# MLP up projection of a two-layer diffusion trunk: two separate two-bank PSUM tiles for blocks A and B in place of the two halves of one

## The chip, the cores and the metric

The kernel runs on one NeuronCore of one Trainium2 chip, in one launch. The metric is the device time of one execution in microseconds. Three runs of the kernel before took 1686.57 us in the median (1686.32 to 1688.69). All matrix products are made in three passes of float32r operands (below), all sums in float32.

## The reference

Two layers of a trunk process 512 latent tokens and 128 context tokens of width 1024. Each layer has a token mixer (differential attention in layer 0, neighbourhood attention in layer 1) and an MLP with squared ReLU. Each sub-layer is modulated, gated and closed by a layer norm; the part that matters here is the MLP:

```python
def modulate(x, shift, scale):
    return x * (1 + scale) + shift

def sq_relu_mlp(h, w1, w2):
    return jnp.square(jax.nn.relu(h @ w1)) @ w2

# in each layer, for context (xp) and latent tokens (xs) alike
y = sq_relu_mlp(modulate(xs, ms[:, 3], ms[:, 4]), w_mlp1[i], w_mlp2[i])
xs = layer_norm(ALPHA * xs + ms[:, 5] * y, ln_g[i, 1], ln_b[i, 1])
```

w1 is 1024 x 4096 and w2 4096 x 1024. The modulation's vectors (shift, scale, gate) are SiLU(cond) times a 1024 x 6144 matrix per layer.

## The kernel before

**Three passes.** Every float32 product is split in hi and lo parts, and `mm3` (lines 119 to 123) issues three matmuls for one 128-deep step: hi x hi, hi x lo, lo x hi. The results build up in PSUM. A 128x512 float32 result is one bank of 2 KB per partition.

**PSUM.** There are eight banks. Two pools, `psA` and `psB` (lines 77 and 78), hold one buffer of `[128, 1024]` each, two banks, under the tag S; `S()` (line 149) hands out the two in turn by a counter `turn`. The other four banks are a ring of one-bank tiles M. `halves()` (line 145) takes one S tile and returns its two banks as two blocks. The framework makes waits from what is read and written in a tile.

**Weights.** They come in quarters of a chunk: 256 rows by 512 columns, a 512 KB DMA on SyncE's queue into one of three raw tiles rw. `conv` (line 184) makes the hi part on ScalarE (wh, line 190) and the lo part (wl, line 192) on VectorE for one half, and for the other on VectorE or, from the first down projection on, on GpSimd. Five converted quarters fit (RING). When the last matmul has used a quarter (`used`, `done`), the next conversion is issued.

**The MLP** is `rest` (line 1200). Four groups (`gr`) of 1024 hidden features each are done in order: up projection in two chunks (`c`) of 512 features, then the down projection of the group. An up chunk has four blocks of 128 features over the 512 latent tokens (`ff`, features on the partitions), and one block C for the 128 context tokens over all 512 features (`nat`). The first two blocks run one after the other into M tiles. The other two, here A and B, and C are staggered (`STAGGER`, line 38): pairs (block, quarter) in the order A0 B0 C0 A1 A2 B1 C1 A3 B2 C2 B3 C3. A quarter of A, B or C is six matmuls. The first chunk of each layer is done otherwise, so seven chunks per layer take this path.

**Read-out.** When a block's quarter 3 is issued, `act` (line 1216) evacuates it: ScalarE makes relu (r, line 1213), VectorE squares it with a second read of the PSUM block (r, line 1214), then `split` makes the operands of the down projection: uhi on ScalarE (line 128), ulo on VectorE (line 129). C goes the same way into rc, and is transposed later.

**Fillers on VectorE.** In layer 0, VectorE also works out layer 1's modulation: 96 products jk of 128x1024 (line 289), two for each 512 KB tile wm that SyncE loads two tiles ahead. `aside` (line 1239) steps this generator after a block's read-out, and the down projection steps it too. In group 0 `aside` scales rows of X instead (line 1041).

**Order.** TensorE's order is that of the code, since it is scheduled by hand. The framework orders the other engines' instructions and the queues by itself.

Of the kernel before, what the change touches and what calls it, by code (L numbers as in the profile page):

```python
# [66 lines left out]
class Net:  # L67
# [1132 lines left out]
    def rest(self, l, X, first):  # L1200
# [3 lines left out]
        with self.tc.tile_pool(name=f"mlp{l}", bufs=1) as pool:  # L1204
# [11 lines left out]
            def act(us, k, src, cs):  # L1216
                r = pool.tile([P, NL], F32, tag="r", name=self.nm("r"), bufs=2)[:, : cs.stop - cs.start]
                op = square(r, src)
                self.split(us[0][:, k, cs], us[1][:, k, cs], r)
                return op  # L1220

            def act_ctx(us, c, src):
                r = pool.tile([P, NL], F32, tag="rc", name=self.nm("rc"), bufs=1)
                op = square(r, src)

                def tr():
                    tp = self.M()
                    for k in range(4):
                        nc.tensor.transpose(tp[:, P * k : P * k + P], r[:, P * k : P * k + P], self.idf)
                    ks = slice(4 * c, 4 * c + 4)  # L1230
                    self.split(us[0][:, ks, NL:], us[1][:, ks, NL:], tp.rearrange("p (a b) -> p a b", b=P))

                wait.append(tr)
                return op
# [4 lines left out]
            def aside(op, x=0):  # L1239
                if gr and x < 2:  # L1240
                    next(mods, None)
                if gr == 0:
                    self.scale(X, len(vec), vec_g, op)
                    vec.append(0)
                elif gr == 1 and len(vec) < 2 * NTT:
                    self.shift(X, len(vec) - NTT, vec_b)
                    vec.append(0)

            for gr in range(4):
                us = [pool.tile([P, KT, NT], F32R, tag=t, name=self.nm(t)) for t in ("uhi", "ulo")]  # L1250
                for c in range(2):
                    n = C0 + 8 + 4 * gr + c
                    if gr == 0 and c == 0:
                        for f in range(4):
                            act(us, f, first[f], slice(0, CUT))
                        for f in range(4):
                            m = self.M()[:, : NT - CUT]
                            self.ff(n, f, CUT, NT, m)
                            act(us, f, m, slice(CUT, NT))
                        gate = self.gate_tiles(pool, l, 1)  # L1260
                        vec_g, vec_b = self.ln_tiles(pool, l, 0)
                        st = self.sml.tile([P, NTT, 2, 6], F32, tag="st", name=self.nm("st"), bufs=2)
                        continue
                    for f in range(2):
                        m = self.M()
                        self.ff(n, f, 0, NL, m)
                        aside(act(us, 4 * c + f, m, slice(0, NL)))
                    while wait:
                        wait.pop()()
                    ms = [*self.halves(), self.M()]  # L1270
                    for x, k in STAGGER:
                        if x < 2:
                            self.ff(n, 2 + x, 0, NL, ms[x], 2 * k, 2 * k + 2)
                        else:
                            self.nat(hT, 4, n, ms[x], 0, 512, 2 * k, 2 * k + 2, k == 0)
                        if k == 3:
                            aside(act(us, 4 * c + 2 + x, ms[x], slice(0, NL)) if x < 2 else act_ctx(us, c, ms[x]), x)
                if gr < 3:
                    for n in range(2):
                        self.pool_lo = 1  # L1280
                        for t in range(NTT):
                            m = self.M()
                            self.nat(us, t, C0 + 10 + 4 * gr + n, m, 0, 512)
                            if n == 0 and t == 1:
                                wait.pop()()
                            self.add_gated_sb(pool, X, t, n, m, gate, gr == 0, nc.gpsimd)
                            next(mods, None)
# [173 lines left out]
```

## Time and profile before

| what | value |
|---|---|
| median of three runs | 1686.57 us (1686.32 to 1688.69) |
| the profiled execution | 1688.53 us, of it span 1686.8 us |
| TensorE busy (PE) / weight loads (PEld) | 1606.5 us (95%) / 1388.0 us (82%) |
| VectorE / ScalarE / GpSimd busy | 1081.2 / 687.9 / 293.0 us |
| mean granted TensorE clock | 0.989 |

The span is counted from the first to the last instruction. In the profile's rows "L121 PE MATMUL S<-hhi,wh" is the matmul of line 121 into a tile S from tiles hhi and wh; "128*128 128x512" is the array and the result. A group's row ends with busy time, mean time of one in ns, and the idle time of the engine ahead of its instructions with the one that ended it. Rows of the order of time begin with start and length in us; the idle time ahead stands in brackets. A matmul's length (0.39 us for 512 columns) is longer than the distance of two starts, as they are pipelined; pace is read from the starts.

### The profile page before, as it was taken

How to read it: one execution, taken by the hardware profiler on the slowest of the kernel's cores; microseconds unless marked ns; L12 is line 12 of the kernel's file. 1: busy time of each engine (PE TensorE's matmuls, PEld its weight loads, DVE VectorE, ACT ScalarE, POOL GpSimd, SP SyncE). 2: the span in 40 equal slices, each digit the busy share in tenths (PEclk: the TensorE clock that was granted, in tenths of full speed). 3: DMA queues.
4: the chain of work that ended last, by engine and by line, in shares of the span. 5: the costliest groups of instructions: out<-in, count | busy, mean ns of one | idle time of the engine just before them, and what ended most of it. 6: DMA issues, size and time to landing. Idle time of an engine off the chain costs nothing. (4 is left out here: it accounts for less than half of the span.)

```text
span 1686.8 us, 23934 instructions
## 1 busy us (share of the span) xinstructions
PE 1606.5 (95%) x9074; PEld 1388.0 (82%) x9074; DVE 1081.2 (64%) x2174; ACT 687.9 (41%) x1398; POOL 293.0 (17%) x236
## 2 busy tenths in 40 slices
PE   8999999899999999999999999998899999999997
PEld 6888989787977778787788999987797878778776
DVE  4788778875659779688366777768654632232336
ACT  2556545744722322313245655554552232231322
POOL 0000000000003246255101011000000224324310
PEclk9999999999999999999999999999999999999999
DMA  8432234331424445444225343444041322221211
GB/s 343 147 122 95 90 118 150 115 113 55 164 86 162 168 142 177 151 161 143 71 88 175 121 136 122 137 137 162 15 149 63 113 72 78 75 75 51 100 51 62
DMA packets 60932, 200.59 MB, mean 119 GB/s; under 512 B 7716, under 2 KB 14354, under 8 KB 59922
## 3 DMA queue, kind: packets, MB, share of 16 engines
q1 hardware_dynamic: 55186, 175.09, 30.4%
q0 software_dynamic: 5632, 23.99, 4.0%
q8 instruction: 71, 1.16, 0.3%
q14 instruction: 43, 0.35, 0.1%
HBM read 186.41 MB, written 7.40 MB: 115 GB/s over the span
## 5 line engine op out<-in xcount | busy, mean ns | idle before, releaser
L190 ACT CAST wh<-rw 128x1024 fp32r<-128x1024 f32 x192 | 199.7, 1053 | 398.1 <-PE M L123 318.3
L192 DVE TENSOR_TENSOR wl<-rw,wh 128x512 fp32r<-128x512 f32 x288 | 224.0, 813 | 148.0 <-ACT wh L190 146.9
L121 PE MATMUL M<-wh,hhi 128*128 128x256 f32 (+1 forms) x752 | 244.4, 325 | 6.4 <-DVE red L266 2.2
L121 PE MATMUL M<-wh,uhi 128*128 128x512 f32 x640 | 250.1, 391 | 0.0
L123 PE MATMUL M<-wh,ulo 128*128 128x512 f32 x640 | 249.1, 389 | 0.0
L122 PE MATMUL M<-wl,uhi 128*128 128x512 f32 x640 | 249.1, 389 | 0.0
L123 PE MATMUL M<-wh,hlo 128*128 128x256 f32 (+1 forms) x752 | 240.2, 319 | 5.8 <-DVE hlo L129 5.6
L122 PE MATMUL M<-wl,hhi 128*128 128x256 f32 (+1 forms) x752 | 239.3, 318 | 0.0
L192 POOL TENSOR_TENSOR wl<-rw,wh 128x512 fp32r<-128x512 f32 x96 | 173.9, 1821 | 324.1 <-ACT wh L190 323.7
L123 PE MATMUL M<-hhi,wl 128*128 128x320 f32 (+2 forms) x544 | 189.0, 347 | 1.9 <-DVE wl L192 1.9
L121 PE MATMUL M<-hhi,wh 128*128 128x320 f32 (+2 forms) x544 | 189.5, 348 | 0.8 <-ACT wh L190 0.6
L122 PE MATMUL M<-hlo,wh 128*128 128x320 f32 (+2 forms) x544 | 188.3, 346 | 0.3 <-DVE hlo L129 0.3
L123 PEld LDWEIGHTS M<-wh,hlo 128*128 128x128 f32 x752 | 144.9, 193 | 18.6 <-DVE hlo L129 9.9
L121 PEld LDWEIGHTS M<-wh,hhi 128*128 128x128 f32 x752 | 145.1, 193 | 18.1 <-DVE red L266 2.5
L122 PEld LDWEIGHTS M<-wl,hhi 128*128 128x128 f32 x752 | 145.3, 193 | 8.6
L1111 DVE TENSOR_TENSOR tmp<-M,gate 128x512 f32<-128x512 f32 x80 | 55.0, 687 | 134.8 <-PE M L123 132.3
L289 DVE SCALAR_TENSOR_TENSOR jk<-wm,cb 128x1024 bf16<-128x1024 f32 x96 | 140.5, 1464 | 1.2
L123 PEld LDWEIGHTS M<-wh,ulo 128*128 128x128 f32 x640 | 120.1, 188 | 25.1
L122 PEld LDWEIGHTS M<-wl,uhi 128*128 128x128 f32 x640 | 120.2, 188 | 24.6
L121 PEld LDWEIGHTS M<-wh,uhi 128*128 128x128 f32 x640 | 120.2, 188 | 24.7
L121 PE MATMUL S<-hhi,wh 128*128 128x512 f32 (+1 forms) x288 | 108.4, 376 | 21.1 <-DVE r L1214 21.1
L123 PEld LDWEIGHTS M<-hhi,wl 128*128 128x128 f32 x544 | 102.7, 189 | 12.5 <-DVE wl L192 3.9
(280 smaller groups left out, 2869.9 us busy)
## 6 DMA issues: line engine op xcount, KB each, us to landing
rw<-in_w SPq DMA_DIRECT2D x192, 512.0 KB, 4.0
wm<-in_wmodT SPq DMA_DIRECT2D x48, 512.0 KB, 3.5
rw<-in_wmod SPq DMA_DIRECT2D x32, 512.0 KB, 4.5
E<-in_bias POOLq DMA_DIRECT2D x32, 384.0 KB, 4.9
wm<-in_wmod SPq DMA_DIRECT2D x7, 1024.0 KB, 11.4
Q<-Q SPq DMA_DIRECT2D x16, 320.0 KB, 3.7
gate<-gates POOLq DMA_DIRECT2D x6, 512.0 KB, 5.1
X<-in_xT SPq DMA_DIRECT2D x8, 320.0 KB, 11.7
```

What stands on the lines that cost most here:

```text
L121: te.matmul(out, sh, mh, start=start, stop=False)
L122: te.matmul(out, sh, ml, start=False, stop=False)
L123: te.matmul(out, sl, mh, start=False, stop=stop)
L190: keep(nc.scalar.copy(hi, r))
L192: keep(eng.tensor_tensor(lo[:, k], r[:, k], hi[:, k], ALU.subtract))
L289: op = nc.vector.scalar_tensor_tensor(jk, ws[t], 1.0, cb[:, x, :], ALU.mult, ALU.mult, accum_out=mc[:, t, x : x + 1])
L1111: nc.vector.tensor_tensor(tmp, m, gate[t // 4][:, cs], ALU.mult)
```

## The change

```diff
@@ -1267,7 +1267,7 @@
                     while wait:
                         wait.pop()()
-                    ms = [*self.halves(), self.M()]
+                    ms = [self.S()[:, :512], self.S()[:, :512], self.M()]
                     for x, k in STAGGER:
                         if x < 2:
                             self.ff(n, 2 + x, 0, NL, ms[x], 2 * k, 2 * k + 2)
```

Before, A and B were the two banks of one S tile, and successive chunks took the two S buffers in turn. Now A is the first bank of one S buffer and B the first bank of the other, in every chunk. Matmuls, read-outs, conversions and loads are the same in number, size and operands, and TensorE's order is the same.

On TensorE, at the end of A's quarter 3 and the start of B's quarter 2 (second chunk of group 2 in layer 0; S with its number is the tile), with the semaphores waited for. Before:

```order
L121 MATMUL S_7099<-hhi,wh_6980 128x512
L122 MATMUL S_7099<-hlo,wh_6980 128x512
L123 MATMUL S_7099<-hhi,wl_6981 128x512
L121 MATMUL S_7099<-hhi,wh_6944 128x512 [waits DVE_49]
L122 MATMUL S_7099<-hlo,wh_6944 128x512
L123 MATMUL S_7099<-hhi,wl_6945 128x512
```

Now:

```order
L121 MATMUL S_7103<-hhi,wh_6984 128x512
L122 MATMUL S_7103<-hlo,wh_6984 128x512
L123 MATMUL S_7103<-hhi,wl_6985 128x512
L121 MATMUL S_7104<-hhi,wh_6948 128x512
L122 MATMUL S_7104<-hlo,wh_6948 128x512
L123 MATMUL S_7104<-hhi,wl_6949 128x512
```

The order is the same; A and B have two tile numbers, and the wait for VectorE at B's quarter 2 is gone. The same holds in all 14 chunks. Some later matmuls name a wait for a wl, or for VectorE at a down projection's first matmul, which they did not name before, because the wait at B's quarter 2 had covered it.

On VectorE, from A's square to rc in the same chunk. Before:

```order
L1214 SCALAR_TENSOR_TENSOR r_7163<-S_7099,r_7163 128x512
L129 TENSOR_TENSOR ulo_6820<-r_7163,uhi_6819 128x512
L289 SCALAR_TENSOR_TENSOR jk_7168,mc_103<-wm_7054,cb 128x1024
L289 SCALAR_TENSOR_TENSOR jk_7170,mc_103<-wm_7054,cb 128x1024
L192 TENSOR_TENSOR wl_7187<-rw_7015,wh_7186 128x512
L1214 SCALAR_TENSOR_TENSOR r_7199<-S_7099,r_7199 128x512
L129 TENSOR_TENSOR ulo_6820<-r_7199,uhi_6819 128x512
L289 SCALAR_TENSOR_TENSOR jk_7204,mc_103<-wm_7090,cb 128x1024
L192 TENSOR_TENSOR wl_7217<-rw_7124,wh_7216 128x512
L289 SCALAR_TENSOR_TENSOR jk_7206,mc_103<-wm_7090,cb 128x1024
L1214 SCALAR_TENSOR_TENSOR rc_7223<-M_7100,rc_7223 128x512
```

Now:

```order
L1214 SCALAR_TENSOR_TENSOR r_7168<-S_7103,r_7168 128x512
L129 TENSOR_TENSOR ulo_6823<-r_7168,uhi_6822 128x512
L289 SCALAR_TENSOR_TENSOR jk_7173,mc_103<-wm_7058,cb 128x1024
L192 TENSOR_TENSOR wl_7192<-rw_7019,wh_7191 128x512
L289 SCALAR_TENSOR_TENSOR jk_7175,mc_103<-wm_7058,cb 128x1024
L1214 SCALAR_TENSOR_TENSOR r_7204<-S_7104,r_7204 128x512
L192 TENSOR_TENSOR wl_7222<-rw_7129,wh_7221 128x512
L129 TENSOR_TENSOR ulo_6823<-r_7204,uhi_6822 128x512
L289 SCALAR_TENSOR_TENSOR jk_7209,mc_103<-wm_7094,cb 128x1024
L1214 SCALAR_TENSOR_TENSOR rc_7228<-M_7105,rc_7228 128x512
L289 SCALAR_TENSOR_TENSOR jk_7211,mc_103<-wm_7094,cb 128x1024
```

The first wl has moved ahead of the second jk, the second wl ahead of B's ulo, and rc ahead of the last jk. The chunks of groups 1 and 2 in layer 0 change in this way, and the first of group 3 in a like one, with the last steps of the modulation; in groups 1 and 2, ScalarE's cast wh for that second wl moves ahead of B's uhi, and on SyncE's queue a load of rw ahead of a load of wm. All other chunks keep their order.

## The prediction

> **What bounds the kernel now.** I read the page first (shares of the span and costliest groups), then the list of waits, then the order of time around one of the waits. The first three rows are the page's, the next two the list of waits, the last the page of line 1214, in the part on who waited for it.
>
> ```profile
> PE 1606.5 (95%) x9074; PEld 1388.0 (82%) x9074; DVE 1081.2 (64%) x2174; ACT 687.9 (41%) x1398; POOL 293.0 (17%) x236
> ...
> L121 PE MATMUL S<-hhi,wh 128*128 128x512 f32 (+1 forms) x288 | 108.4, 376 | 21.1 <-DVE r L1214 21.1
> L123 PE MATMUL M<-hhi,wl 128*128 128x320 f32 (+2 forms) x544 | 189.0, 347 | 1.9 <-DVE wl L192 1.9
> ...
> PEld S L121 <- DVE r L1214: 27.0, 14, 2.1
> PE S L121 <- DVE r L1214: 21.1, 14, 1.7
> ```
>
> TensorE is busy for 95% of the span; the next engine, VectorE, for 64%. What TensorE does not do at full pace is what the span is made of. The largest idle time that section 5 shows before any of its groups is 21.1 us before matmuls into a tile S, all ended by VectorE's squared ReLU (line 1214), in 14 places. Fourteen is the number of staggered pieces: 4 MLP groups x 2 chunks x 2 layers, less the first chunk of each layer, which takes another path. The order of time shows one such place in layer 0:
>
> ```profile
> 478.40 0.39 PE L122 MATMUL S<-hlo,wh 128*128 128x512 f32 x1
> 478.63 0.39 PE L123 MATMUL S<-hhi,wl 128*128 128x512 f32 x1
> ...
> 479.12 0.60 ACT L1213 ACTIVATE r<-S 128x512 f32<-128x512 f32 x1 [0.36 <-PE S L123]
> 480.00 0.68 DVE L1214 SCALAR_TENSOR_TENSOR r<-S,r 128x512 f32<-128x512 f32 x1
> ...
> 480.74 0.50 PE L121 MATMUL S<-hhi,wh 128*128 128x512 f32 x1 [1.72 <-DVE r L1214]
> 481.07 0.39 PE L122 MATMUL S<-hlo,wh 128*128 128x512 f32 x1
> ```
>
> Block A's last matmul starts at 478.63. ScalarE and VectorE read A's half of S, and only when VectorE is through (480.68) does block B go on (480.74). B's data need none of it: its weights are those that A's third step has already used, and its half of S is written by nobody else. So what B waits for is the tile, not a value.
>
> **The change part by part.** (1) *What it removes.* Matmuls of 512 columns start 0.23 us apart (478.40, 478.63). Here 2.11 us pass (478.63 to 480.74), so 1.88 are lost, and the matmul behind starts 0.33 later instead of 0.23, another 0.10: 1.98 us. The idle time shown (1.72) is less, since a matmul's own 0.39 overlaps the next one's start. A second kind of place, here in the third group of layer 0:
>
> ```profile
> 707.60 0.39 PE L123 MATMUL S<-hhi,wl 128*128 128x512 f32 x1
> 709.47 0.50 PE L121 MATMUL S<-hhi,wh 128*128 128x512 f32 x1 [1.47 <-DVE r L1214]
> 709.80 0.39 PE L122 MATMUL S<-hlo,wh 128*128 128x512 f32 x1
> ```
>
> 1.87 - 0.23 = 1.64, and 0.33 - 0.23 = 0.10: 1.74 us. Two of the 14 are of the first kind (the first group of each layer, where a weight conversion stood ahead of the square on VectorE) and 12 of the second: 2 x 1.72 + 12 x 1.47 = 21.1, the idle time in the group's row, so the count is right. The loss is 2 x 1.98 + 12 x 1.74 = **24.8 us**. With two tiles B's third step has no reason to wait, as the rows of the new order show. All of it lies on the path, because TensorE has nothing else to do there: its instructions stand in one fixed order.
>
> (2) *What it adds.* Each block asks for a tile of its own and leaves its second bank unused. Twice as many requests per chunk, on the same two buffers: A always takes one, B the other, where whole chunks alternated before. So A's first step must wait until A of the chunk before is read out. Between B's last step and its next first step lie 6 matmuls of C, 48 of the next chunk's first two blocks and 6 of A, 60 x 0.23 = 13.8 us; B's read-out ends, by the slowest chain worked out below, 3.9 us after B's last start. Cost nothing; if the cover were gone, at most the 1.74 us per chunk that stand there now. The requests at the end of layer 0 (the early V blocks) change buffers, since 14 requests flip the turn by an even number where 7 flipped it by an odd one. Between their read-out and the next work on these buffers, the first scores, the written order has seven other blocks of matmuls: nothing.
>
> (3) *What it moves.* Layer 1 keeps its order on VectorE, ScalarE and the queues. In layer 0 five chunks (two each in groups 1 and 2, the first of group 3) carry the modulation's products (jk, in pairs), and there the order changes: conversion (wl) moves ahead of the second jk, and B's ulo stands behind the next wl. On SyncE's queue a weight load (rw) moves ahead of a modulation load (wm) in four of them; wm is loaded two pairs ahead of its use, and no jk of this trace waits for a DMA, so that costs nothing (without this cover a load's median 3.5 us each, section 6 of the page). This is where a gain can be lost, so I work through the tightest case, a chunk that is followed by the down projection (709.47 on), which needs ulo at once:
>
> ```profile
> 708.72 0.69 DVE L1214 SCALAR_TENSOR_TENSOR r<-S,r 128x512 f32<-128x512 f32 x1 [0.23 <-ACT r L1213]
> 710.10 0.69 DVE L129 TENSOR_TENSOR ulo<-r,uhi 128x512 fp32r<-128x512 f32 x1 [0.69 <-ACT uhi L128]
> 710.71 1.22 DVE L289 SCALAR_TENSOR_TENSOR jk<-wm,cb 128x1024 bf16<-128x1024 f32 x1
> ...
> 713.65 0.69 DVE L192 TENSOR_TENSOR wl<-rw,wh 128x512 fp32r<-128x512 f32 x1 [0.45 <-ACT wh L190]
> 714.58 0.69 DVE L1214 SCALAR_TENSOR_TENSOR r<-S,r 128x512 f32<-128x512 f32 x1 [0.23 <-ACT r L1213]
> 715.96 0.69 DVE L129 TENSOR_TENSOR ulo<-r,uhi 128x512 fp32r<-128x512 f32 x1 [0.69 <-ACT uhi L128]
> ...
> 717.71 1.77 DVE L192 TENSOR_TENSOR wl<-rw,wh 128x512 fp32r<-128x512 f32 x1
> ...
> 723.00 2.19 DVE L289 SCALAR_TENSOR_TENSOR jk<-wm,cb 128x1024 bf16<-128x1024 f32 x1
> ...
> 712.57 1.05 ACT L190 CAST wh<-rw 128x1024 fp32r<-128x1024 f32 x1 [2.50 <-PE M L123]
> ...
> 713.70 1.81 POOL L192 TENSOR_TENSOR wl<-rw,wh 128x512 fp32r<-128x512 f32 x1 [4.08 <-ACT wh L190]
> 716.95 1.98 POOL L192 TENSOR_TENSOR wl<-rw,wh 128x512 fp32r<-128x512 f32 x1 [1.45 <-ACT wh L190]
> 721.90 2.21 POOL L1119 TENSOR_TENSOR X<-X,tmp 128x512 f32<-128x512 f32 x1 [2.97 <-DVE tmp L1111]
> ...
> 715.04 0.39 PE L121 MATMUL M<-wh,uhi 128*128 128x512 f32 x1
> ...
> 720.26 0.39 PE L123 MATMUL M<-wh,ulo 128*128 128x512 f32 x1
> ```
>
> Three facts: a wl or a jk that starts under a GpSimd instruction lasts until that has ended and then its own time (717.71 and 723.00 above, 1.77 and 2.19 against 0.69 and 1.22). GpSimd converts the other half of each quarter, for 1.8 to 2.0 us. The down projection's matmul on B's ulo starts at 720.26, its weight load one start earlier, at 720.03.
>
> Now take 1.74 us off TensorE's times after 707.60. The cast of 712.57 starts at 710.83 and ends at 711.88. VectorE is through with the first jk at 711.93, does its wl till 712.62; GpSimd converts till 713.7. The second jk starts under it and ends at 713.7 + 1.22 = 714.9; B's square, which could have started at 712.84, ends at 715.6. The next cast, behind C's last step, ends near 714.5, GpSimd's half at 716.5, VectorE's wl behind it at 717.2, then ulo at **717.9**. It is wanted at 720.03 - 1.74 = **718.29**. So 0.4 us are left of what were 3.4 (716.65 against 720.03). I cost this at nothing, but it is thin: if my chain is 1 us short, each of the two such chunks with jk and a down projection behind them (groups 1 and 2) stalls 0.6 us, 1.2 in all; if jk and wl both meet GpSimd once more (about 1 us each), 2 x 1.6 = 3.2. The other three moved chunks are followed by work on older tiles and lie easier. Bounds of this term: 0 to +3.2 us; I take 0.2.
>
> VectorE stays later than before behind such a chunk, but it catches up; the down projection as a whole is unchanged, and TensorE's clock is full in all of it:
>
> ```profile
> 566.66:596.14 29.48, 28.00 (x124) 22.85 (x125) 19.93 (x30) 9.97 (x15) 7.36 (x5) 1.00 0.41 143
> 596.14:680.00 83.86, 82.39 (x365) 67.89 (x365) 73.38 (x88) 18.41 (x23) 45.30 (x23) 1.00 0.48 163
> 1359.68:1389.16 29.48, 28.00 (x125) 22.85 (x125) 9.51 (x14) 9.96 (x15) 7.18 (x5) 1.00 0.21 72
> ```
>
> The columns are the stretch, its length, then busy time of PE, PEld, DVE, ACT and POOL, the granted clock, and the DMA share. From stall to stall of one group (566.66 to 596.14) VectorE works 19.93 of 29.48 us; without the stall 19.93 of 27.74, 72%. In the 83.86 us with the down projection in it, 73.38, 88%, and of 82.12 it would be 89%. So there is room in every stretch of layer 0, and much in layer 1 (9.51 us).
>
> (4) *A wait that stays.* At 544.85 and 547.67 TensorE waits for wl (most of the 1.9 us of the page's third row), behind a run of VectorE work without a pause that begins at 508.76:
>
> ```profile
> 544.15 0.39 PE L122 MATMUL M<-hlo,wh 128*128 128x512 f32 x1
> 544.85 0.50 PE L123 MATMUL M<-hhi,wl 128*128 128x512 f32 x1 [0.31 <-DVE wl L192]
> ...
> 546.11 0.40 PE L122 MATMUL M<-hlo,wh 128*128 128x512 f32 x1
> 547.67 0.50 PE L123 MATMUL M<-hhi,wl 128*128 128x512 f32 x1 [1.16 <-DVE wl L192]
> ...
> 508.76 0.69 DVE L1111 TENSOR_TENSOR tmp<-M,gate 128x512 f32<-128x512 f32 x1 [1.61 <-PE M L123]
> ```
>
> From start to start less 0.23 that is 0.47 and 1.33, with 0.1 behind each 2.0 us. The run begins with VectorE waiting 1.61 us for TensorE; if TensorE comes 1.98 us earlier, all of it does. I leave the wait as it is: bounds -2.0 (it vanishes) and +2.0 (the one gain ahead of it, 1.98, is eaten).
>
> **Sum.** -24.8 + 0.2 = -24.6 us. The profiled execution took 1688.53 us, 1.7 more than its span of 1686.8; the three runs have the median 1686.57. Nothing outside the span changes, so the profile should show a span near 1662.2, and the median should be 1686.57 - 24.6 = **1662.0 us**. The likeliest case's own range is 24.8 less 3.2 and 2.0, to 24.8 plus 2.0: 1659.8 to 1667.0.
>
> **The rivals.** *A, VectorE becomes the bound in the modulation's chunks.* If the new order makes ulo or wl late by as much as the stall was, the five moved chunks of layer 0 give back 5 x 1.74 = 8.7 us: 1662.0 + 8.7 = 1670.7. For it: 0.4 us of slack in the chain above, and the wait at 544.85, which shows that wl can be late. Against it: 28% of VectorE free, and three of the five have no consumer near. Chance 0.09.
>
> *B, nothing gained.* TensorE would find another thing to wait for at the same place, or the wait would stay on the tile: 1686.6. For it speaks little: B's third step uses weights that A's third step used without a wait, and the new order has no wait there. Chance 0.03. The Trainium skill has a case of this kind (TensorE: Matmul & The Clock Gate, section "HAM oscillation — how this bites in real kernels"): in a kernel that kept TensorE fed, adding PSUM double-buffering gave no further gain. By that this change would give nothing; the 14 waits above show that this kernel's TensorE is not fed at these points, so the trace disagrees.
>
> *C, slower: the clock.* Place: the two MLP stages, from which the pauses are taken. The granted clock of TensorE is the last but two of the columns:
>
> ```profile
> 42.00:420.00 378.00, 361.19 (x2612) 321.48 (x2612) 292.40 (x767) 206.43 (x508) 13.85 (x25) 0.97 0.34 112
> 420.00:452.00 32.00, 28.68 (x190) 27.58 (x189) 20.39 (x42) 26.25 (x64) 3.13 (x6) 0.95 0.35 131
> 452.00:850.00 398.00, 385.97 (x1713) 317.35 (x1712) 297.57 (x399) 101.20 (x130) 134.85 (x70) 1.00 0.41 141
> 1236.00:1630.00 394.00, 383.45 (x1717) 317.94 (x1716) 146.56 (x203) 105.56 (x141) 112.83 (x74) 1.00 0.24 83
> ```
>
> For it: the clock is not always full here. If TensorE without pauses were granted 0.95 in these 792 us, as it was from 420 to 452, they would last 792 x (1/0.95 - 1) = 41.7 us longer: 1703.7. It decides at 792 x (1/c - 1) = 24.6, a clock of 0.97. Against it: in the 83.86 us above TensorE runs without a pause but one, at 1.00, and the stages with less are those in which it idles more (361.19 busy of 378, against 385.97 of 398). Chance 0.02. The same page of the Trainium skill (section "What's actually happening") says that idleness throttles the array and activity releases it, and the four rows agree; by that, C can't happen.
>
> **How the numbers follow.** Forecast 0.86, A 0.09, B 0.03, C 0.02. A measurement of this kernel can tell about 0.2%, 3.4 us, from no change. Forecast and A are both faster by far more: 0.95; same 0.03; slower 0.02. The range reaches from a little under the forecast's own low end, 1659.5, to 1668.5, part of the way to A; it leaves out most of A, B and C (0.14) and some of the forecast's edges.
>
> **What would show it.** In the profile after: the row of matmuls into S with its 21.1 us idle before and "DVE r L1214" gone from the waits of PE and PEld; stall-to-stall stretches of one group 27.7 us long instead of 29.48; VectorE's busy time as before. A step is wrong if TensorE shows new waits for "DVE ulo L129" at a down projection's start (rival A's), for "DVE wl L192" beyond the 1.9 us of now, or the clock of the MLP stages is below 1.00 (C). The forecast as a whole is wrong if TensorE's starts across A's end are still 1.9 us apart.

## The result, and the profile after

The changed kernel takes **1660.93 us** in the median (1657.39 to 1663.16, 4 runs); the kernel before, in 4 runs beside it, 1687.63. The ratio is **0.9838** (95% interval 0.9817 to 0.986), 27.3 us less by the ratio (23.6 to 30.9). The forecast was 1662.0, its range 1659.5 to 1668.5. Of the profiled execution's 1663.16 us the span is 1661.3, 25.5 less than before.

The first two rows of the page after and the row of section 5 that still has an idle time ended by wl:

```profile
span 1661.3 us, 23941 instructions
PE 1604.7 (97%) x9074; PEld 1391.2 (84%) x9074; DVE 1081.3 (65%) x2174; ACT 688.6 (41%) x1398; POOL 290.3 (17%) x236
...
L123 PE MATMUL M<-hhi,wl 128*128 128x320 f32 (+2 forms) x544 | 188.5, 347 | 2.0 <-DVE wl L192 2.0
```

The same work, busy for the same time (TensorE 1604.7 us against 1606.5), in a shorter span. The matmuls into S with 21.1 us of idle time ahead are no longer among the costliest groups, and no wait of TensorE for line 1214 is left in the list of waits. The place where block A ends and B goes on, in the order of time after (second chunk of group 2, layer 0, where 1.87 us passed before):

```profile
700.54 0.39 PE L123 MATMUL S<-hhi,wl 128*128 128x512 f32 x1
700.77 0.39 PE L121 MATMUL S<-hhi,wh 128*128 128x512 f32 x1
701.00 0.39 PE L122 MATMUL S<-hlo,wh 128*128 128x512 f32 x1
...
701.03 0.60 ACT L1213 ACTIVATE r<-S 128x512 f32<-128x512 f32 x1 [0.32 <-PE S L123]
701.66 0.69 DVE L1214 SCALAR_TENSOR_TENSOR r<-S,r 128x512 f32<-128x512 f32 x1 [0.23 <-ACT r L1213]
```

0.23 us from start to start: B runs on while A is read out (701.03 to 702.35). The stretches of time after, with the columns of the prediction (stretch, length, busy time and count of PE, PEld, DVE, ACT, POOL, granted clock, DMA share, GB/s): the two pieces between stalls that the prediction measured, then the MLP stages of both layers:

```profile
563.28:590.98 27.70, 27.70 (x125) 22.92 (x124) 20.00 (x31) 10.07 (x14) 6.71 (x4) 1.00 0.51 175
590.98:673.08 82.10, 82.10 (x366) 67.96 (x365) 73.57 (x89) 18.53 (x22) 44.65 (x22) 1.00 0.47 159
450.00:840.00 390.00, 388.44 (x1736) 321.97 (x1735) 299.78 (x404) 102.07 (x132) 132.14 (x70) 1.00 0.43 146
1223.00:1604.00 381.00, 381.00 (x1716) 318.17 (x1715) 146.63 (x203) 105.55 (x141) 112.96 (x74) 1.00 0.25 86
```

29.48 has become 27.70 and 83.86 has become 82.10, where 27.74 and 82.12 were worked out. TensorE is busy without a gap in both, and in all of layer 1's MLP, at a clock of 1.00. From one chunk's transpose of C (line 1229) to the next chunk's, the distance shrinks by 1.67 to 1.77 us, in each of the 12 steps; over the first pause of each layer, from a matmul ahead of it to the next transpose of C, it shrinks by 2.02. That is 12.5 us in layer 0 and 12.6 in layer 1, 25.2 in all before rounding.

### The profile page after: what moved, and what is told of

The parts are those of the page before. It is cut to its first block, busy times and chain, and to the rows that moved or that the text cites. A ratio compares the mean times of both kernels' runs of the same rounds, so it can differ in the third digit from the quotient of the medians.

```text
span 1661.3 us, 23941 instructions
## 1 busy us (share of the span) xinstructions
PE 1604.7 (97%) x9074; PEld 1391.2 (84%) x9074; DVE 1081.3 (65%) x2174; ACT 688.6 (41%) x1398; POOL 290.3 (17%) x236
## 5 line engine op out<-in xcount | busy, mean ns | idle before, releaser
L289 DVE SCALAR_TENSOR_TENSOR jk<-wm,cb 128x1024 bf16<-128x1024 f32 x96 | 145.9, 1520 | 1.0
L123 PEld LDWEIGHTS M<-wh,ulo 128*128 128x128 f32 x640 | 120.1, 188 | 25.2
L121 PEld LDWEIGHTS M<-hhi,wh 128*128 128x128 f32 x544 | 102.2, 188 | 10.1 <-ACT wh L190 0.7
```

Of the source, the lines that this page charges most:

```text
L121: te.matmul(out, sh, mh, start=start, stop=False)
L123: te.matmul(out, sl, mh, start=False, stop=stop)
L289: op = nc.vector.scalar_tensor_tensor(jk, ws[t], 1.0, cb[:, x, :], ALU.mult, ALU.mult, accum_out=mc[:, t, x : x + 1])
```

## The experiments

Each kernel is compared with the kernel before on the same chip. "The change" is the kernel after; a difference in us is the ratio's, of some 1685 us.

### Which chunks the gain comes from

The two tiles in only the five chunks that carry the modulation's products, and in only the other nine:

```diff
-                    ms = [*self.halves(), self.M()]
+                    ms = [self.S()[:, :512], self.S()[:, :512], self.M()] if l == 0 and (gr in (1, 2) or (gr == 3 and c == 0)) else [*self.halves(), self.M()]
```

Five chunks:

> Two tiles only in the five chunks of layer 0 in which VectorE also makes the modulation's products (groups 1 and 2, first chunk of group 3); one tile in the other nine. Theory (the wait is on the tile, and nothing takes its place): 5 x 1.74 = 8.7 us less than before, 14 - 5 = 9 waits of TensorE for VectorE's square left, 2 x 1.72 + 7 x 1.47 = 13.7 us of shown idle time. Rival A (VectorE gives it back in these chunks): time as before, and new waits for ulo or wl in their place.

The nine others (the two sides of that condition exchanged):

> Two tiles in the other nine chunks, one tile in the five with the modulation's products. Theory: 2 x 1.98 + 7 x 1.74 = 16.1 us less than before, 5 waits left, 7.4 us of shown idle time; with the run of the five it adds up to the whole change. Rival A: the whole gain of the change, some 25 us, is here.

The row of the list of waits (us in total, times, longest), with five chunks changed:

```profile
PE S L121 <- DVE r L1214: 13.7, 9, 1.7
```

and with nine:

```profile
PE S L121 <- DVE r L1214: 7.4, 5, 1.5
```

Measured: 0.9955 (0.9939 to 0.9971), 7.6 us less, and 0.9909 (0.9893 to 0.9925), 15.3 less. So the gain goes with the number of chunks, 1.5 and 1.7 us for each, and the five in which the prediction saw a danger give theirs like the rest. By rival A these five would have given nothing; it is out. The traces say it more sharply than the times: from the first transpose of C to the last chunk's, layer 0 took 342.20 us before and 333.40 with the five chunks changed, 8.8 less, which is 1.76 for each, and layer 1 took 340.00 in both.

### The gain is the tile, not the pool

A, B and C each take a one-bank tile from the ring M; no S buffer is used.

```diff
-                    ms = [*self.halves(), self.M()]
+                    ms = [self.M(), self.M(), self.M()]
```

> A and B take one-bank tiles from the ring M of four, like C; S is not used in these chunks. Theory (any separate tile will do, one bank is enough): some 25 us less than before, within 2 us of the change. Rival (the ring of four becomes too short with five blocks in flight): TensorE waits for the square of a block read out earlier, up to 1.7 us in each of 14 chunks, time near before.

Measured: 0.9853 (0.9836 to 0.9871), 24.8 us less, and the list has no wait of TensorE for the square of a block (line 1214). What matters is that A and B are not one tile. Which buffers they come from does not: four one-bank buffers are enough for the five blocks of a chunk.

### The read-out made longer

If the 14 waits are waits for A's read-out, a longer read-out must cost its length in the kernel before and nothing with two tiles. The relu of A and B is made twice; the output stays the same:

```diff
-            def square(r, src):
-                nc.scalar.activation(r, src, AF.Relu)
+            def square(r, src, twice=False):
+                for _ in range(2 if twice else 1):
+                    nc.scalar.activation(r, src, AF.Relu)
```

With one tile, as before:

> The kernel before (one tile) with ScalarE's relu of A and of B made twice, 0.60 us more in each read-out. Theory (TensorE's loss is the read-out's length): each of 14 waits is 0.60 us longer, 8.4 us more than before, 21.1 + 8.4 = 29.5 us of shown idle time. If the read-out's length did not set the loss: as before.

With two tiles, as in the change:

> The changed kernel (two tiles) with the same relu made twice for A and B. Theory: TensorE does not wait for it, so as the change, within 2 us; in the two chunks of layer 0 that are followed by a down projection and carry the modulation's products, 0.6 us of the 1.1 us that ulo of B had left in the changed kernel's trace are used up. If the read-out is only just hidden, a wait for ulo shows there.

With two tiles: 0.9853 (0.9836 to 0.9869), as the change without the second relu, and no wait for ulo appears; the read-out is off the path there. With one tile 1.0129 (1.011 to 1.0148), **21.7 us longer, where 8.4 were expected**. The waits are as expected (list of waits):

```profile
PE S L121 <- DVE r L1215: 29.4, 14, 2.1
```

The rest is in the order of time behind the first pause, and in two stretches (columns as above; the one behind the pause that began at 477.23, the other behind an equally long one):

```profile
477.23 0.39 PE L123 MATMUL S<-hhi,wl 128*128 128x512 f32 x1
479.72 0.79 PE L121 MATMUL S<-hhi,wh 128*128 128x512 f32 x1 [2.10 <-DVE r L1215]
480.31 0.63 PE L122 MATMUL S<-hlo,wh 128*128 128x512 f32 x1
480.74 0.63 PE L123 MATMUL S<-hhi,wl 128*128 128x512 f32 x1
```

```profile
479.70:483.10 3.40, 3.38 (x8) 2.70 (x9) 1.70 (x2) 0.62 (x1) 0.00 (x0) 0.50 0.48 154
599.70:603.10 3.40, 3.40 (x15) 2.82 (x16) 2.75 (x4) 0.90 (x2) 0.00 (x0) 1.00 0.48 154
```

Behind the first, TensorE is granted half its clock: 8 matmuls, 0.43 us apart, instead of 15. It happens after 8 of the 14 pauses, each for 3.41 us, of which half is lost: 8 x 1.7 = 13.6 us. Such a piece at half clock is called a fall below. With the longer pauses (12 x 0.62 and 2 x 0.38, 8.2 us) that makes 21.8, the measured time.

### When does the clock fall?

Pauses of 1.87 and 2.11 us in the kernel before never did it, pauses of 2.49 did it 8 times of 14. So the length of the pause was varied: the second relu over half the columns, and three relus over all. In `square`:

```diff
-                nc.scalar.activation(r, src, AF.Relu)
+                if twice:
+                    nc.scalar.activation(r[:, :256], src[:, :256], AF.Relu)
+                nc.scalar.activation(r, src, AF.Relu)
```

> The kernel before with one relu more over half of the columns of blocks A and B. A relu over 512 columns took 0.60 us more where it was made twice, and one over 256 columns should take some 0.38 us more, so each of the 14 pauses of TensorE becomes 1.87 + 0.38 = 2.25 us from start to start, beside 2.49 us where the relu was made twice over all columns. By the read-out alone: 14 x 0.38 = 5.3 us longer than before. If a pause of this length lets the clock fall to half after 8 of 14, as it did at 2.49 us, some 14 us more come on top, 19 us in all, and eight stretches of matmuls 0.43 us apart are seen. I hold the first for likelier, since 1.87 to 2.11 us never did it in the kernel before.

```diff
-                nc.scalar.activation(r, src, AF.Relu)
+                for _ in range(3 if twice else 1):
+                    nc.scalar.activation(r, src, AF.Relu)
```

> The kernel before with the relu of blocks A and B made three times: each of the 14 pauses becomes 1.87 + 2 x 0.60 = 3.1 us from start to start. By the read-out alone: 14 x 1.2 = 17 us longer than before. If the clock falls by the length of the pause, it should now fall after all or nearly all of the 14, each for some 3.4 us, which cost about 1.7 us each where it fell after 8: 17 + 14 x 1.7 = 41 us. If 8 of 14 was by chance of where the pause fell and the length does nothing to it: 17 + 14 = 31 us.

Measured with half a relu more: 1.0091 (1.0075 to 1.0107), 15 us longer, pauses of 2.28 us, and 7 falls. The case that I held for likelier, no fall and 5.3 us, is wrong; the other, 8 falls and 19 us, is near. With two relus more: 1.0165 (1.0151 to 1.0179), 28 us longer, pauses of 3.12 us, and only **4** falls. So a longer pause does not mean more falls, and both expectations for that kernel (41 and 31 us) miss.

What decides shows when the stretches are cut where the falls begin. In the kernel with half a relu more they begin at 479.82, 681.20 and 797.26 us; the distances, 201.38 and 116.06, are 59 and 34 times 3.413, and every change of the clock in each of these traces lies on such a grid. In that grid, for that kernel, a pause that lies whole in one stretch (476.51 to 478.79), and one that is cut by the border at 565.15 (564.58 to 566.86):

```profile
476.41:479.82 3.41, 1.52 (x7) 0.93 (x6) 3.07 (x5) 1.83 (x4) 0.00 (x0) 1.00 0.23 55
479.82:483.23 3.41, 3.41 (x10) 2.66 (x9) 0.65 (x2) 0.00 (x0) 0.00 (x0) 0.50 0.25 99
...
565.15:568.56 3.41, 1.70 (x7) 1.42 (x8) 2.08 (x4) 1.52 (x3) 1.44 (x1) 1.00 0.67 226
568.56:571.98 3.42, 3.42 (x17) 2.82 (x16) 2.69 (x5) 1.74 (x3) 0.90 (x1) 1.00 0.35 111
```

In a stretch, count as lost what lies between two starts beyond a matmul's own pace (0.23 us for 512 columns). Over the MLP stages of the change, the kernel before and all kernels run so far, 63 stretches at full clock lose 1.5 us or more. Of the 40 with at most 1.99 us lost none is followed by half clock; of six with 2.05 to 2.08 three are; of the 17 with 2.10 or more, all 17. The pauses of 3.12 us in the kernel with three relus were mostly cut by a border: most come in pairs 30.7 to 30.9 us apart, nine stretches, so that a pair is cut alike.

The rule was formed after these runs, so it was put to a new one, with a pause length not tried (the extra relu over 384 columns):

> The kernel before with one relu more over 384 of the 512 columns of blocks A and B: each of the 14 pauses 0.53 us longer, some 2.38 us from start to start, 2.15 us lost. The rule read off the earlier runs, put to the test: the clock falls to half for one stretch of 3.413 us of a fixed grid when at least 2.10 us of the stretch before it were lost, and never when 1.99 or less were; in between either may be. So a pause falls only if it lies nearly whole in one stretch of the grid: by chance (3.41 - 2.15 + 2 x 0.1) / 3.41 = 43%, about 6 of the 14, at places that the length of the pause alone does not tell. Time by the read-out alone 14 x 0.53 = 7 us longer than before, with 6 falls of 1.7 us some 17 us; 12 to 21 us with 3 to 8 falls. If the length of the pause alone decided, all 14 would fall or none: 31 or 7 us. The rule is wrong if a pause that lies whole in a stretch is followed by full pace, or one cut in the middle by half pace.

Measured: 1.0117 (1.0088 to 1.0147), 19.7 us longer, with 9 falls of 14. Two pauses of the same length, 681.50 to 683.88 whole in its stretch but for the last 0.04 us, and 713.02 to 715.41 cut at 714.56:

```profile
680.43:683.84 3.41, 1.46 (x7) 0.88 (x5) 1.38 (x2) 2.14 (x3) 1.77 (x1) 1.00 0.77 298
683.84:687.26 3.42, 3.38 (x8) 2.71 (x9) 2.72 (x4) 0.62 (x1) 0.00 (x0) 0.50 0.50 155
711.15:714.56 3.41, 2.26 (x10) 1.53 (x9) 0.69 (x1) 2.07 (x3) 1.30 (x1) 1.00 0.32 129
714.56:717.98 3.42, 2.57 (x11) 2.14 (x12) 2.60 (x5) 0.69 (x2) 0.48 (x1) 1.00 0.51 153
717.98:721.39 3.41, 3.41 (x17) 2.83 (x16) 2.26 (x4) 2.30 (x4) 1.74 (x1) 1.00 0.34 89
```

All eight stretches with 2.12 to 2.27 us lost were followed by half clock, all with 1.9 or less by full clock, and one with 2.03, between the bounds, by half. The count, 9, is a little over the 3 to 8 that were named; the rule itself held at every place. By it 6.7 + 9 x 1.7 = 22.0 us, inside the measured interval of 14.8 to 24.8. For the three relus it gives 17.0 + 4 x 1.7 = 23.8, less than the 25.5 to 30.2 measured. In the profiled execution the rule's sum is there: from the first pause to the end of the last, layer 0 took 344.30 us before and 357.50 with three relus, layer 1 342.11 and 352.27, together 23.4 longer. So the excess does not lie between these pauses in that execution. Outside them TensorE's work is the same, and it took 995.2 to 1000.9 us in the five traces with pauses, longest with three relus; the other executions were not traced, so that rest stays open.

### Another way to the same gain: cover in place of a second tile

One S tile as before, but B's quarter 2 issued ahead of A's quarter 3, so that C's last two quarters lie between A's end and B's last quarter:

```diff
-STAGGER = (0, 0), (1, 0), (2, 0), (0, 1), (0, 2), (1, 1), (2, 1), (0, 3), (1, 2), (2, 2), (1, 3), (2, 3)
+STAGGER = (0, 0), (1, 0), (2, 0), (0, 1), (0, 2), (1, 1), (2, 1), (1, 2), (0, 3), (2, 2), (2, 3), (1, 3)
```

> One tile as before, but the stagger written so that both last steps of C stand between A's end and B's last step (B2 ahead of A3, then C2 C3 B3). The wait on A's read-out stays in the program, at B3, 12 matmuls (2.7 us) behind A's last start; the read-out was over 1.87 to 2.11 us behind it. Theory (what was lost is only the time in which TensorE had nothing before the wait): some 25 us less than before, as with two tiles. Rival (two tiles have a worth of their own, such as reads and writes in separate buffers): no more than half of it. B's read-out now ends 1.4 us later against the down projection; in layer 0 that may show as a wait for ulo of under 1 us in two chunks.

Measured: 0.9891 (0.9872 to 0.991), 18.4 us less: most of the gain, not all. The waits on S are gone, but the list has two new ones:

```profile
PE M L121 <- ACT uhi L128: 3.1, 2, 1.6
...
PE M L123 <- DVE ulo L129: 0.7, 2, 0.4
```

and the order of time shows the first at the down projection behind group 2 (group 1's is alike):

```profile
711.61 0.39 PE L123 MATMUL M<-wh,ulo 128*128 128x512 f32 x1
713.55 0.50 PE L121 MATMUL M<-wh,uhi 128*128 128x512 f32 x1 [1.55 <-ACT uhi L128]
...
708.73 2.31 DVE L289 SCALAR_TENSOR_TENSOR jk<-wm,cb 128x1024 bf16<-128x1024 f32 x1
710.97 0.68 DVE L1214 SCALAR_TENSOR_TENSOR rc<-M,rc 128x512 f32<-128x512 f32 x1
711.57 0.68 DVE L192 TENSOR_TENSOR wl<-rw,wh 128x512 fp32r<-128x512 f32 x1
712.17 0.68 DVE L1214 SCALAR_TENSOR_TENSOR r<-S,r 128x512 f32<-128x512 f32 x1
```

B is now the last block, and on VectorE its square stands behind jk, C's square and a wl, so uhi is late. The two waits cost 2.1 us each by starts, with the slower starts behind them; the second had its 2.1 us in one stretch of the grid, and seven matmuls behind it ran at half pace (1.4 us). The two waits for ulo, behind group 0 of each layer, cost 0.6 us each: 6.8 us in all, beside the 6.4 that lack to the ring's 24.8. I had expected under 1 us in the chunks of groups 1 and 2, from TensorE's order, without the work that stands ahead of the square on VectorE.

### The wait that the change leaves

The change, with three steps of the modulation moved from the first down projection to its end, so that VectorE has less to do ahead of the wait for wl:

```diff
-                            next(mods, None)
+                            if gr or n == 0 or t < 2:
+                                next(mods, None)
```

> The changed kernel, with three steps of the modulation's products left out of the first down projection's last rows and made at the end, where three steps were free. VectorE has 3 x 2.4 = 7.3 us less in the run that ends in TensorE's wait for wl near 545 us. Theory for the wait that stayed (VectorE is behind in that run): the wait, 2.1 us by starts, goes, and the time falls by 2 us against the change. Rival (the wait comes from the conversion's own chain, cast and GpSimd): it stays.

The place in the change, in the order of time:

```profile
542.30 0.39 PE L122 MATMUL M<-hlo,wh 128*128 128x512 f32 x1
543.10 0.50 PE L123 MATMUL M<-hhi,wl 128*128 128x512 f32 x1 [0.41 <-DVE wl L192]
...
544.38 0.39 PE L122 MATMUL M<-hlo,wh 128*128 128x512 f32 x1
545.92 0.50 PE L123 MATMUL M<-hhi,wl 128*128 128x512 f32 x1 [1.15 <-DVE wl L192]
```

With the steps moved, the same matmuls, a little earlier in that trace:

```profile
542.74 0.39 PE L123 MATMUL M<-hhi,wl 128*128 128x512 f32 x1
543.42 0.39 PE L123 MATMUL M<-hhi,wl 128*128 128x512 f32 x1
544.10 0.39 PE L123 MATMUL M<-hhi,wl 128*128 128x512 f32 x1
```

0.68 us, three matmuls' pace, from one to the next: the wait is gone. The time was 0.9841 (0.982 to 0.9863), not to be told from the change. So both were timed again on one chip; the change:

> The change itself again, beside the next kernel on one chip: 0.984 of the time before, as in its own runs (26.7 us shorter).

and with the steps moved:

> The change, with three steps of the modulation moved from the first down projection to its end, as before but timed in more rounds beside the change: the wait of TensorE at wl near 545 us is gone, which is 2.0 us by starts, so 2 us shorter than the change, if nothing is moved behind it.

0.9852 (0.9837 to 0.9868), 1660.89 us, against 0.9841 (0.9827 to 0.9855), 1659.08 us. The difference of the medians, 1.8 us, is near what the wait lasted, but the intervals overlap. The traces settle it for the stage: from the first transpose of C in layer 0 to the last chunk's, with the wait between them, the two traces of the change took 331.68 and 331.62 us and the two with the steps moved 329.50 each, 2.1 to 2.2 less. That the whole time falls by it is not shown, since the rest of the span took 1324.8 to 1329.6 us in these four traces. No kernel here beat the change by more than that.

## Why the prediction was right

**What bounds it (right).** The 14 waits were on the tile: with two tiles they go, with five or nine chunks they go in proportion, and a longer read-out costs nothing once they are gone. Since TensorE is the bound and its order is fixed, each removed us comes off the end.

**(1) What it removes (right to 0.4 us).** 24.8 us were worked out from starts, 25.2 were found chunk by chunk (2.02 where 1.98 was worked out, 1.67 to 1.77 where it was 1.74); the span fell by 25.5, the median, by the ratio, by 27.3 (23.6 to 30.9), and by 25.0 (22.3 to 27.5) when the change was run again. The idle time shown, 21.1, would have been 4.1 short.

**(2) What it adds (right).** No wait for an S buffer appeared, and the ring did as well.

**(3) What it moves (right in direction, the size off).** The chain was to leave 0.4 us for B's ulo at the down projection behind group 2. In the trace after, from VectorE's first jk behind A's read-out on, with GpSimd's and ScalarE's part and the matmul that wants it:

```profile
703.65 1.22 DVE L289 SCALAR_TENSOR_TENSOR jk<-wm,cb 128x1024 bf16<-128x1024 f32 x1
704.82 0.69 DVE L192 TENSOR_TENSOR wl<-rw,wh 128x512 fp32r<-128x512 f32 x1
705.43 2.31 DVE L289 SCALAR_TENSOR_TENSOR jk<-wm,cb 128x1024 bf16<-128x1024 f32 x1
707.67 0.68 DVE L1214 SCALAR_TENSOR_TENSOR r<-S,r 128x512 f32<-128x512 f32 x1
708.28 1.17 DVE L192 TENSOR_TENSOR wl<-rw,wh 128x512 fp32r<-128x512 f32 x1
709.37 0.68 DVE L129 TENSOR_TENSOR ulo<-r,uhi 128x512 fp32r<-128x512 f32 x1
...
706.45 1.06 ACT L190 CAST wh<-rw 128x1024 fp32r<-128x1024 f32 x1 [0.75 <-PE M L123]
...
704.87 1.79 POOL L192 TENSOR_TENSOR wl<-rw,wh 128x512 fp32r<-128x512 f32 x1 [2.28 <-ACT wh L190]
707.59 1.31 POOL L192 TENSOR_TENSOR wl<-rw,wh 128x512 fp32r<-128x512 f32 x1 [0.93 <-ACT wh L190]
...
711.42 0.39 PE L123 MATMUL M<-wh,ulo 128*128 128x512 f32 x1
```

These times are 7.06 us earlier than those of the prediction's chain, which had this chunk's stall taken off already. Up to B's square each step came within 0.2 us of it: first jk's end 704.87 (worked out 704.87), second jk's end 707.74 (707.84), square's end 708.35 (708.5). Then GpSimd's half took 1.31 us instead of the 1.98 that I had carried over from a row of before, VectorE's wl behind it ended 0.7 earlier, and ulo ended at 710.05, wanted by a weight load one start ahead of 711.42, at 711.20: **1.15 us of slack instead of 0.4**. The term of 0.2 us was mis-sized by its whole; it measured 0. The same GpSimd operation lasts 1.79 us where jk runs beside it and 1.31 where the square of a PSUM block does for the first half of it. The prediction read 1.8 to 2.0 us for it, but the trace before has shorter ones: 1.29 us at 517.71, beside a VectorE product that reads a PSUM block (line 1111, 517.49), and 1.34 at 800.28, behind a square of S, with small VectorE products beside it. The new order puts the square of B beside its start, so these were the nearer rows.

**(4) The wait that stays (right).** 0.57 and 1.31 us by starts with 0.11 behind each, 2.1 us, against 2.0; both bounds of 2.0 were too careful.

**The rivals.** A and B are out by the chunks and the waits. (The 28% of VectorE free that was named against A holds for the shorter piece; in the longer one, by the prediction's own rows, 11% was free.) C is out: the clock of the MLP stages is 1.00. Its row from 420 to 452 (0.95) was the wrong kind of evidence: the experiments show that pauses lower the clock, and the change takes pauses away. The kernel before stood closer to that than anything in its profile tells. Its worst stretch,

```profile
478.25:481.66 3.41, 1.69 (x8) 1.10 (x7) 2.88 (x4) 1.72 (x3) 0.00 (x0) 1.00 0.15 47
```

lost 1.99 us, and the clock fell from about 2.05 on.

## What to carry to other kernels

When a matmul waits for the read-out of a block that it does not touch, look whether both are parts of one tile: waits go by tile here, and a request per block cost no work and no order on TensorE. Price such a stall from start to start, with the slower start behind it, and look on the other engines for what the earlier start will reorder, step by step, before giving the gain away. When a pause of TensorE is made longer or shorter, ask also whether it crosses about 2.1 us within 3.4: there its price jumped by 1.7 us in this kernel.

## What the runs showed of the hardware

**The clock falls on a fixed grid.** Half clock came in pieces of 3.413 us (or several in a row, outside the MLP stages) that begin on a grid of that length in each of the traces, and within the MLP it followed where 2.1 us or more of the stretch before were lost to TensorE. So two equal pauses differ by 1.7 us in price, by where a border falls. The Trainium skill (TensorE: Matmul & The Clock Gate, section "What's actually happening") has the length and says that it runs freely, and the runs agree; it gives half clock to an idle window of about 3.4 us, and here 2.1 us lost of 3.41 was enough, with matmuls in the same stretch. The measurement decides: in the 23 stretches of the first runs with 2.05 us or more lost, 20 were followed by half clock, and even the one that lost most lost 2.89 us and not all of the 3.41.

**A pause costs more than it shows.** The first start behind a pause of a full-clock stretch is followed at 0.33 instead of 0.23 us, as the orders of time show (480.74 to 481.07 before, 543.10 to 543.44 after), 0.1 us on top of each pause.
